# Low products behind their hi products in the attention part, and later joins at the end of each half

## The chip, the cores and the metric

The kernel runs on one core of a Trainium2 chip. The metric is the device time in microseconds, the median of several runs. One further execution was recorded by the hardware profiler, and the profile's rows are from that one.

## The reference

A bidirectional encoder of two layers over 256 tokens of width 2048, in float32:

```python
for l in range(DEPTH):                      # DEPTH = 2
    h = rms_norm(x, norm1_g[l])
    q, k, v, gu, gv = jnp.split(h @ w_in[l], splits, axis=-1)
    q = apply_rope(rms_norm(q...), cos, sin); k = apply_rope(rms_norm(k...), cos, sin)
    attn = banded_window_attention(q, k, v, sink[l])        # 8 heads of 128, 2 of k and v, |i-j| <= 128
    sgu = chunked_spatial_gating(gelu(gu), gelu(gv), ...)   # layer norm, 128x128 mixing per head, times gu
    mixed = concatenate([rms_norm(attn, ...), rms_norm(sgu, ...)])
    x = x + mixed @ w_o[l]
    x = x + conv_gated_ffn(rms_norm(x, norm2_g[l]), w_up[l], conv_w[l], conv_b[l], w_down[l])
# conv_gated_ffn: a = 3-tap convolution of h @ w_up along the tokens; g, u = split(a); (silu(g) * u) @ w_down
```

D_FF is 5632, so w_up and w_down carry most of the matmuls.

## The kernel before

Every matrix product is made of three matmuls in a rounded float format. Both factors are split: `hi` is the value rounded (a copy on ScalarE, ACT), `lo` is the rest (a subtraction on VectorE, DVE). The weight's hi part is multiplied with the activation's hi and lo part (the two "hi products"), the weight's lo part with the activation's hi part (the "low product").

Weights come in chunks of 128 x 2048 (1 MB) over SyncE's (SP) queue into `raw`, are split by `split_weights` (hi at L154, lo at L142) in pieces of a given step, and are used by one block of matmuls on TensorE (PE). There are four raw buffers, three hi buffers, three lo buffers, three PSUM accumulators `mm` and two small PSUM buffers `tp`. A buffer is let go when its last reader is done, and each engine takes its instructions in the order in which they stand in its own stream.

Four kinds of block touch the change.

- `rows_by_cols` (L181): 4 chunks of 128 rows of the weight against two token halves, 16 hi products and then 8 low products, each 512 wide. It makes the input projections (`in_rows`), the output projection (`out_rows`) and the up projection (`up_rows`).
- `unit` (L325, L330): four units a layer make the gating input gu with tokens along the free axis. A unit has two weight chunks, so two hi and two lo buffers; 32 hi products (512 wide) and then 32 low products (256 wide). Steps handed to it are run between its low products.
- The attention itself runs as a list of steps that blocks and units take in (`take`, and `let_in` for steps that wait in a list): scores (L368 to L370 on PE into a `tp` buffer, read by DVE at L558 for the masked maximum, exponentials on ACT at L580, scaling at L588), transposes of the probabilities (L596), their split (L362 on ACT, L363 on DVE) and the value products (again L368 to L370), copied out at L605.
- `direct` (L209) and `seven` (L269, L270, L275) make the down projection: plain blocks of 16 hi and 8 low products, and blocks for two column groups with seven products in place of eight. Feed-forward rows are treated in two halves; after the up projection of a half come its down blocks.

Rows of the up projection leave PSUM through `leave`: ACT scales them (L914), copies them as 16-bit words (L916), SP turns them by DMA, and some blocks later ACT joins them (L495), they are convolved (L896 on ACT, L897 and L900 on DVE), the gate's go through silu (L936), the up rows are multiplied in (L944) and the product is split (L356, L357). How many blocks later is set by `after(n, step)`: the step goes through `n` further calls of `let_in` in which it only moves up.

The order of instructions in each engine's stream is not the program's order: a scheduler works it out from priorities (`urgent()` raises them) and its own costs, and `issue_after(latest())` ties a step behind the latest matmul. A change of the program's order can so move instructions on all engines.

Of the kernel before, what the change touches and what calls it, by code (L numbers as in the profile page):

```python
# [25 lines left out]
NK = D // P  # L26
NF = DFF // P
W = 512
KB = 4
# [37 lines left out]
def encoder(ctx: ExitStack, tc: tile.TileContext, xT, x, w_in, w_gu, w_o, w_up, w_down, wsT, pcol, prow, rope, out):  # L67
# [18 lines left out]
    def ev():  # L86
        return sl([P, 2, SEQ])
# [77 lines left out]
    def after(n, step):  # L165
        waiting.append(step if n == 0 else lambda: after(n - 1, step))

    def let_in():
        for step in waiting[:]:
            waiting.remove(step)  # L170
            with tc.issue_after(latest()), urgent():
                step()


    def rows_by_cols(ps, acts, src, first, last, raw=None, apart=False, step=4 * W):

        hi, lo = split_weights(src, raw, step)

        def product(m, kk, part):
            w = (hi if part < 2 else lo)[:, kk * W : (kk + 1) * W]  # L180
            nc.tensor.matmul(  # L181
                ps[m], acts[kk][:, part % 2, m * P : (m + 1) * P], w,
                start=first and kk == 0 and part == 0, stop=last and kk == KB - 1 and part == 2,
            )

        if apart:
            for m in range(2):
                for kk in range(KB):
                    for part in range(3):
                        product(m, kk, part)  # L190
            return
        for kk in range(KB):
            for m in range(2):
                product(m, kk, 0)
                product(m, kk, 1)
            if kk == 1:
                let_in()
        for kk in range(KB):
            for m in range(2):
                product(m, kk, 2)  # L200
# [103 lines left out]
    def take(steps):  # L304
        for step in steps:
            with tc.issue_after(latest()):
                step()


    def unit(acts, w, steps=()):  # L310
        ps = mm()
        his, los = [], []
        for b in range(0, NK, UB):
            h, lo = split_weights(w[:, b * UW : (b + UB) * UW], None, 2 * W)
            his.append(h)
            los.append(lo)

        def tile_of(tiles, k, i):
            c = k % UB * UW + i * P
            return tiles[k // UB][:, c : c + P]  # L320

        for k in range(NK):
            for i in range(2):
                x1 = acts[k].rearrange("p a b -> p (a b)")
                nc.tensor.matmul(ps[:, i, :], tile_of(his, k, i), x1, start=k == 0, stop=False)  # L325
            if k == 5:
                let_in()
        for k in range(NK):
            for i in range(2):
                nc.tensor.matmul(  # L330
                    ps[:, i, :SEQ], tile_of(los, k, i), acts[k][:, 0, :], start=False, stop=k == NK - 1
                )
            if k == 0:
                take(steps)
        return ps


# [344 lines left out]
    NB = NK // KB  # L682
    for l in range(DEPTH):
        pc, qk = params
        acts = hT

        def in_rows(ps, c, b):
            src = w_in[l, c, :, b * KB * W : (b + 1) * KB * W]
            raw = first_raws.pop(0) if l == 0 and first_raws else None
            step = 2 * W if raw is None else W  # L690
            rows_by_cols(ps, acts[b * KB : b * KB + KB], src, b == 0, b == NB - 1, raw, step=step)


        psk, psq = mm(), mm()
# [27 lines left out]
        atts = []  # L722
# [41 lines left out]
        first = group_steps(0, psq)  # L764
        first()
        ps = chunk(1, [[sent_keys], [turned_keys, first], [], [first]] if l else [[], [], [sent_keys, first], [turned_keys]])
# [8 lines left out]
        for i in range(2):  # L775
# [4 lines left out]
            ps = chunk(3 + i, between[i])  # L780
# [73 lines left out]
        gates = []  # L854
# [6 lines left out]
        def out_rows(half, c, r):  # L861
            t = mm()
            ps = [t[:, m, :] for m in range(2)]
            for b in range(2):
                src = w_o[l, c, :, (half * 2 + b) * KB * W : (half * 2 + b + 1) * KB * W]
                rows_by_cols(ps, (atts, gates)[half][b * KB : b * KB + KB], src, b == 0, b == 1, step=4 * W if half else 2 * W)
            residual(ps, c, r)

        ra = inv_rms_cols(acca, D // 2, "a")
# [36 lines left out]
            src = w_up[l, n * (NF // 4) + j, :, b * KB * W : (b + 1) * KB * W]  # L906
            rows_by_cols([ps[:, m, :] for m in range(2)], acts2[b * KB : b * KB + KB], src, b == 0, b == NB - 1)

        def leave(ps, then):
            halves = []  # L910
            for m in range(2):
                rows = ev().rearrange("p a b -> p (a b)")
                with urgent():
                    nc.scalar.activation(rows, ps[:, m, :], AF.Copy, scale=r2[:, m : m + 1])  # L914
                h = sl([P, 2, 2, SEQ], U16)
                nc.scalar.copy(h, rows.bitcast(U16).rearrange("p (j n b) -> p j b n", j=2, b=2))  # L916
                halves.append(h)
            tall = [sl([P, 4, SEQ], U16) for _ in range(2)]

            def asked():  # L920
                for j in range(2):
                    for m in range(2):
                        half = halves[m][:, j, :, :].rearrange("p b n -> p (b n)")
                        nc.sync.dma_start_transpose(tall[j][:, :, m * P : (m + 1) * P], half)
                after(2, lambda: then(tall))

            waiting.append(asked)

        def gate_and_up(j, ys, mixes):
            gs = []  # L930

            def gate_in(tall):
                for i in range(2):
                    g = together(tall[i])
                    y = convolved(g, 4 * j + 2 * i)
                    nc.scalar.activation(y, y, AF.Silu)  # L936
                    gs.append(y)

            def up_in(tall):
                for i in range(2):  # L940
                    u = together(tall[i])
                    y = gs[i]
                    t = convolved(u, NF + 4 * j + 2 * i)
                    nc.vector.tensor_tensor(out=y, in0=y, in1=t, op=ALU.mult)  # L944
                    for k in range(2):
                        ys.append(split_plain(y[:, k, :]))
                    k = len(ys) - 2
                    if k in FAST[half]:
                        e = mixed(y)
                        waiting.append(lambda e=e, k=k: mixes.__setitem__(k, parts(e, [P, W])))  # L950

            if j == 0:
                pss = [mm(), mm()]
                for b in range(NB):
                    for n in range(2):
                        up_rows(pss[n], n, j, b)
                        if b == NB - 1:
                            leave(pss[n], (gate_in, up_in)[n])
                return
            for n in range(2):  # L960
                ps = mm()
                for b in range(NB):
                    up_rows(ps, n, j, b)
                leave(ps, (gate_in, up_in)[n])

        w_at = 0
        for half, (f0, f1) in enumerate(HALVES):
# [5 lines left out]
            last = f1 == NF  # L973
# [122 lines left out]
```

## Time and profile before

| | |
|---|---|
| median of three runs | 1971.12 us (1969.78 to 1973.15) |
| the profiled execution's time | 1969.81 us |
| its span in the profile | 1968.0 us |
| PE busy | 1954.8 us, 99% |
| DVE busy, ACT busy | 1334.6 us (68%), 1318.1 us (67%) |
| bytes read from HBM | 378.43 MB, 193 GB/s over the span |
| granted PE clock | full in all slices |

A row of the time lines reads: start, duration (both us), engine, line of the kernel, operation, out<-in with shapes, count, and in brackets the idle time of the engine ahead of it with what ended that. In the lists of waits: the waiting engine and line, what it waited for, us in total, times, the longest. The regions around the change: input and output projections and attention of layer 0 from the start to about 250 us, of layer 1 from about 995; the units of layer 0 from about 110 to 165, of layer 1 from about 1103 to 1158; the down blocks of the first half near 480 to 550 in layer 0 and 1460 to 1520 in layer 1.

### The profile page before, as it was taken

Reading aid. Unit: us, or ns where it says so; the run is one execution under the profiler, and the core shown is the slowest. Engines: PE = TensorE matmul, PEld = TensorE weight load, DVE = VectorE, ACT = ScalarE, POOL = GpSimd, SP = SyncE. Lnnn points to the kernel's source line nnn. Section 1 sums busy time; section 2 is a strip of 40 time slices with the busy share of each in tenths; the row PEclk is TensorE's granted clock in tenths of the full one; section 3 lists DMA queues with packets and bytes.
Section 4 is the critical chain, followed back from the end, with each engine's and each line's share of the span. In section 5 each row is a group of like instructions: output and inputs, shape, how many; then the busy total and the mean of one; then the engine's idle time right before and its main releaser. Section 6 shows DMA issues by size and latency. Waiting matters only on the chain.

```text
span 1968.0 us, 22935 instructions
## 1 busy us (share of the span) xinstructions
PE 1954.8 (99%) x8832; PEld 1622.1 (82%) x8832; DVE 1334.6 (68%) x1628; ACT 1318.1 (67%) x1437; POOL 22.9 (1%) x25
## 2 busy tenths in 40 slices
PE   9999999999999999999999999999999999999999
PEld 7878888888788888888888888888888888888887
DVE  6768775666874666688566696756668655666873
ACT  6667487687644777776666774877885456777742
POOL 0000000000000000000000000000000000000000
PEclk9999999999999999999999999999999999999999
DMA  9763486776665677757767546867766667677572
GB/s 373 218 213 141 171 235 190 220 227 195 217 235 187 217 226 223 213 174 246 231 205 221 172 150 203 242 199 222 217 197 218 214 205 223 214 217 224 169 267 86
DMA packets 190733, 414.02 MB, mean 210 GB/s; under 512 B 139424, under 2 KB 140704, under 8 KB 145568
## 3 DMA queue, kind: packets, MB, share of 16 engines
q1 hardware_dynamic: 189904, 411.83, 66.1%
q8 instruction: 69, 1.13, 0.2%
q10 hardware_dynamic: 720, 0.73, 0.1%
q14 instruction: 40, 0.33, 0.1%
HBM read 378.43 MB, written 2.10 MB: 193 GB/s over the span
## 4 chain that ended last, share of the span: by engine, by line
PE 87%; ACT 5%; DMA 3%; DVE 3%; issue 2%; SPq 0%; DVEq 0%; ACTq 0%
PE mm L181 59%; PE mm L209 17%; DMA sl<-sl 3%; PE mm L325 3%; ACT hi L154 2%; PE tp L209 2%; DVE lo L142 2%; PE mm L330 1%; ACT sl L916 1%; PE mm L275 1%; PE mm L270 1%; PE mm L269 1%; ACT sl L914 1%; ACT sl L495 1%; DVE sl L897 0%
## 5 line engine op out<-in xcount | busy, mean ns | idle before, releaser
L142 DVE TENSOR_TENSOR lo<-raw,hi 128x2048 fp32r<-128x2048 f32 (+3 forms) x444 | 839.0, 1904 | 491.0 <-ACT hi L154 442.2
L181 PE MATMUL mm<-hi,sl 128*128 128x512 f32 x3968 | 943.4, 389 | 0.9 <-ACT hi L154 0.8
L154 ACT ACTIVATE hi<-raw 128x2048 fp32r<-128x2048 f32 (+2 forms) x412 | 650.3, 1594 | 364.8 <-PE mm L181 171.7
L181 PEld LDWEIGHTS mm<-hi,sl 128*128 128x128 f32 x3968 | 744.4, 188 | 156.1 <-ACT hi L154 1.7
L181 PE MATMUL mm<-lo,sl 128*128 128x512 f32 x1984 | 491.3, 389 | 0.0
L181 PEld LDWEIGHTS mm<-lo,sl 128*128 128x128 f32 x1984 | 372.1, 188 | 76.9
L209 PE MATMUL mm<-hi,sl 128*128 128x512 f32 x1056 | 250.4, 389 | 1.9 <-ACT hi L154 1.9
L209 PEld LDWEIGHTS mm<-hi,sl 128*128 128x128 f32 x1056 | 198.1, 188 | 43.8 <-ACT hi L154 2.8
L495 ACT COPY sl<-sl 128x1024 uint16<-128x1024 uint16 x98 | 132.5, 1352 | 134.7 <-DMA sl<-sl 134.5
L209 PE MATMUL mm<-lo,sl 128*128 128x512 f32 x528 | 130.4, 389 | 0.0
L209 PEld LDWEIGHTS mm<-lo,sl 128*128 128x128 f32 x528 | 99.1, 188 | 20.5
L896 ACT ACTIVATE sl<-sl,pc 128x256 f32<-128x256 f32 x176 | 95.8, 590 | 1.3
L916 ACT COPY sl<-sl 128x1024 uint16<-128x1024 uint16 x88 | 92.0, 1046 | 2.6
L897 DVE SCALAR_TENSOR_TENSOR sl<-sl,pc 128x255 f32<-128x255 f32 x176 | 77.9, 478 | 8.1 <-ACT sl L896 8.0
L900 DVE SCALAR_TENSOR_TENSOR sl<-sl,pc 128x255 f32<-128x255 f32 x176 | 77.9, 478 | 0.7
L325 PE MATMUL mm<-sl,hi 128*128 128x512 f32 x256 | 63.7, 394 | 1.6 <-ACT sl L784 1.6
L356 ACT ACTIVATE sl<-sl 128x256 fp32r<-128x256 f32 x88 | 31.7, 408 | 46.7 <-DVE sl L944 46.7
L914 ACT ACTIVATE sl<-mm,yr 128x512 f32<-128x512 f32 x88 | 59.7, 678 | 0.0
L325 PEld LDWEIGHTS mm<-sl,hi 128*128 128x128 f32 x256 | 46.8, 188 | 10.6 <-ACT sl L784 1.8
L349 DVE SCALAR_TENSOR_TENSOR sl<-sl,pc 128x256 fp32r<-128x256 f32 x96 | 42.1, 479 | 17.6 <-ACT sl L348 17.4
L348 ACT ACTIVATE sl<-sl,pc 128x256 fp32r<-128x256 f32 x96 | 43.0, 498 | 2.3 <-DMA sl<-in_xT 1.1
L252 ACT ACTIVATE hi<-raw 128x2048 fp32r<-128x2048 f32 x16 | 30.6, 1914 | 19.2 <-PE mm L209 14.1
(144 smaller groups left out, 1062.5 us busy)
## 6 DMA issues: line engine op xcount, KB each, us to landing
raw<-in_w_up SPq DMA_DIRECT2D x176, 1024.0 KB, 5.0
raw<-in_w_down SPq DMA_DIRECT2D x88, 1024.0 KB, 4.8
raw<-in_w_in SPq DMA_DIRECT2D x38, 1024.0 KB, 5.1
raw<-in_w_o SPq DMA_DIRECT2D x32, 1024.0 KB, 5.0
raw<-in_w_gu SPq DMA_DIRECT2D x16, 1024.0 KB, 5.4
sl<-sl SPq DMA_TRANSPOSE x244, 4.3
sl<-in_prow SPq DMA_DIRECT2D x12, 256.0 KB, 7.4
raw<-in_w_in SPq DMA_DIRECT2D x8, 256.0 KB, 5.3
```

The lines of the kernel that those rows point to most:

```text
L142: nc.vector.tensor_tensor(out=lo, in0=part, in1=hi.bitcast(F32), op=ALU.subtract)
L154: nc.scalar.activation(hi[:, cs], raw[:, cs], AF.Copy)
L181: nc.tensor.matmul(ps[m], acts[kk][:, part % 2, m * P : (m + 1) * P], w, start=first and kk == 0 and part == 0, stop=last and kk == KB - 1 ...
L209: nc.tensor.matmul(ps[m], acts[kk][:, part % 2, m * P : (m + 1) * P], w, start=first, stop=done and kk == len(acts) - 1 and part == 2,)
L325: nc.tensor.matmul(ps[:, i, :], tile_of(his, k, i), x1, start=k == 0, stop=False)
L348: nc.scalar.activation(t[:, 0, :], src, AF.Copy, scale=g)
L495: nc.scalar.copy(words, tall.rearrange("p (b a) n -> p b (a n)", b=2))
L896: nc.scalar.activation(t[:, i, :], s[:, i, :], AF.Identity, bias=col(3), scale=col(1))
L897: nc.vector.scalar_tensor_tensor(out=t[:, i, 1:], in0=s[:, i, : SEQ - 1], scalar=col(0), in1=t[:, i, 1:], op0=ALU.mult, op1=ALU.add)
L900: nc.vector.scalar_tensor_tensor(out=t[:, i, : SEQ - 1], in0=s[:, i, 1:], scalar=col(2), in1=t[:, i, : SEQ - 1], op0=ALU.mult, op1=ALU.add)
L914: nc.scalar.activation(rows, ps[:, m, :], AF.Copy, scale=r2[:, m : m + 1])
L916: nc.scalar.copy(h, rows.bitcast(U16).rearrange("p (j n b) -> p j b n", j=2, b=2))
```

## The change

Three edits.

1. In `rows_by_cols`, where `in_turn` is set (all input projections, and the output projection's first half): the two low products of a row group follow its four hi products, instead of all eight low products at the end.
2. In `unit`, the low products go through all 16 rows for the first column half and then for the second, instead of alternating. The first lo buffer's last reader so is the 24th low product instead of the 16th. The steps are taken in after the second low product in both.
3. `leave` gets the number of blocks to wait, which is 3 instead of 2 for the last rows of a half.

```diff
-    def rows_by_cols(ps, acts, src, first, last, raw=None, apart=False, step=4 * W):
+    def rows_by_cols(ps, acts, src, first, last, raw=None, in_turn=False, step=4 * W):
...
         for kk in range(KB):
             for m in range(2):
                 product(m, kk, 0)
                 product(m, kk, 1)
+            if in_turn:
+                for m in range(2):
+                    product(m, kk, 2)
             if kk == 1:
                 let_in()
+        if in_turn:
+            return
         for kk in range(KB):
             for m in range(2):
                 product(m, kk, 2)
...
-        for k in range(NK):
-            for i in range(2):
+        for i in range(2):
+            for k in range(NK):
                 nc.tensor.matmul(
                     ps[:, i, :SEQ], tile_of(los, k, i), acts[k][:, 0, :], start=False, stop=k == NK - 1
                 )
-            if k == 0:
-                take(steps)
+                if i == 0 and k == 1:
+                    take(steps)
...
-            rows_by_cols(ps, acts[b * KB : b * KB + KB], src, b == 0, b == NB - 1, raw, step=step)
+            rows_by_cols(ps, acts[b * KB : b * KB + KB], src, b == 0, b == NB - 1, raw, True, step)
...
-                rows_by_cols(ps, (atts, gates)[half][b * KB : b * KB + KB], src, b == 0, b == 1, step=4 * W if half else 2 * W)
+                rows_by_cols(ps, (atts, gates)[half][b * KB : b * KB + KB], src, b == 0, b == 1, None, half == 0, 4 * W if half else 2 * W)
...
-                after(2, lambda: then(tall))
+                after(wait, lambda: then(tall))
...
-                leave(ps, (gate_in, up_in)[n])
+                leave(ps, (gate_in, up_in)[n], 2 + (j == f1 // 4 - 1))
```

(The branch `apart` of `rows_by_cols`, which nothing called, is gone too.) In the changed kernel the lines from L187 on have other numbers: L209 is L208, L325 is L324, L330 is L329, L349 is L348, L355 to L363 and L368 to L370 one less each, L495 is L494, L558 is L557, L896 is L895.

The streams of three engines move as follows. In the names, `tp_8633`, `tp_8643` hold scores of the second pair of heads' first two heads in layer 1, `tp_8738` those of the next; `lo_8960` is unit 2's second lo chunk and `lo_9084` unit 3's first; `mm_8818` is unit 1's accumulator.

DVE, units of layer 1, before:

```order
L379 TENSOR_TENSOR sl_7908<-sl_7908,sl_8591 128x512 [waits Activation_49]
L349 SCALAR_TENSOR_TENSOR sl_8594<-sl_8589,pc_2444,sl_8594 128x256 [waits Activation_49]
L349 SCALAR_TENSOR_TENSOR sl_8597<-sl_8589,pc_2444,sl_8597 128x256 [waits DMAHW4_49,Activation_49]
L558 ISA sl_8634,nmx_8632<-tp_8633,mask_121,qs_8171 128x256 [waits DMAHW5_49,PE_49]
...
L558 ISA sl_8644,nmx_8632<-tp_8643,mask_121,qs_8171 128x256 [waits DVE_49,PE_49]
...
L558 ISA sl_8739,nmx_8737<-tp_8738,mask_121,qs_8171 128x256 [waits DMAHW7_49,PE_49]
...
L142 TENSOR_TENSOR lo_8960<-raw_8957,hi_8959 128x1024 [waits DMAHW2_49,PE_49]
...
L142 TENSOR_TENSOR lo_9084<-raw_9081,hi_9083 128x1024 [waits DMAHW3_49,PE_49]
```

and in the changed kernel:

```order
L378 TENSOR_TENSOR sl_7908<-sl_7908,sl_8591 128x512 [waits Activation_49]
L142 TENSOR_TENSOR lo_8960<-raw_8957,hi_8959 128x1024 [waits DMAHW2_49,PE_49]
L142 TENSOR_TENSOR lo_8960<-raw_8957,hi_8959 128x1024
L142 TENSOR_TENSOR lo_9084<-raw_9081,hi_9083 128x1024 [waits DMAHW3_49,DVE_49,PE_49]
L142 TENSOR_TENSOR lo_9084<-raw_9081,hi_9083 128x1024
L348 SCALAR_TENSOR_TENSOR sl_8594<-sl_8589,pc_2444,sl_8594 128x256 [waits DMAHW4_49,Activation_49]
L348 SCALAR_TENSOR_TENSOR sl_8597<-sl_8589,pc_2444,sl_8597 128x256 [waits DMAHW5_49,Activation_49]
L557 ISA sl_8634,nmx_8632<-tp_8633,mask_121,qs_8171 128x256 [waits DMAHW6_49]
...
L557 ISA sl_8644,nmx_8632<-tp_8643,mask_121,qs_8171 128x256 [waits DMAHW7_49]
```

The four lo pieces have moved ahead of the L349 pair and of all reads of scores.

PE in the same place, before:

```order
L330 MATMUL mm_8818<-sl_7194,lo_8822 128x256 x2
L330 MATMUL mm_8818<-sl_7233,lo_8822 128x256 x2
L368 MATMUL tp_8738<-sl_8057,sl_8578 128x256
L369 MATMUL tp_8738<-sl_8058,sl_8578 128x256
L370 MATMUL tp_8738<-sl_8057,sl_8579 128x256
```

and in the changed kernel:

```order
L329 MATMUL mm_8818<-sl_7703,lo_8830 128x256
L329 MATMUL mm_8818<-sl_7708,lo_8830 128x256
L329 MATMUL mm_8818<-sl_7711,lo_8830 128x256
L367 MATMUL tp_8738<-sl_8057,sl_8578 128x256
L368 MATMUL tp_8738<-sl_8058,sl_8578 128x256
L369 MATMUL tp_8738<-sl_8057,sl_8579 128x256
```

The scores of the next head stood after the unit's tenth low product; they now stand after its last one.

ACT, down blocks of layer 0's first half, before (`hi_4187` and `hi_4217` belong to the third and fourth plain block, `hi_4385` and `hi_4417` to the last two, `hi_4450` to the second half's first block; `sl_4231` and `sl_4307` are the convolved up rows):

```order
L495 COPY sl_4229<-sl_4079 128x2x512 [waits DMAHW2_49,DMAHW1_49]
L896 ACTIVATE sl_4231<-sl_4229,pc_83 128x256 [waits Activation_49]
L154 ACTIVATE hi_4187<-raw_4185 128x2048 [waits DMAHW6_49,DVE_49,PE_49]
L896 ACTIVATE sl_4231<-sl_4229,pc_83 128x256
L154 ACTIVATE hi_4217<-raw_4215 128x2048 [waits DMAHW7_49,DVE_49,PE_49]
```

and in the changed kernel:

```order
L154 ACTIVATE hi_4385<-raw_4383 128x2048 [waits DMAHW7_49,DVE_49,PE_49]
L292 COPY sl_4280<-mm_4147 128x512 [waits PE_49]
L154 ACTIVATE hi_4417<-raw_4415 128x2048 [waits DMAHW0_49,DVE_49,PE_49]
L494 COPY sl_4305<-sl_4059 128x2x512 [waits DMAHW2_49,DMAHW1_49]
L895 ACTIVATE sl_4307<-sl_4305,pc_83 128x256 [waits Activation_49]
L895 ACTIVATE sl_4307<-sl_4305,pc_83 128x256
L154 ACTIVATE hi_4450<-raw_4448 128x2048 [waits DMAHW1_49,DVE_49,PE_49]
L355 ACTIVATE sl_4315<-sl_4078 128x256 [waits DVE_49]
```

The join of the up rows has moved from ahead of the third block's hi piece to behind the last block's.

More of the change, by code (lines that the diff above doesn't have):

```diff
@@ L184, in product @@
             )
[L186 to L191, printed above, removed]
         for kk in range(KB):
@@ L907, in up_rows, with leave @@
             rows_by_cols([ps[:, m, :] for m in range(2)], acts2[b * KB : b * KB + KB], src, b == 0, b == NB - 1)
-        def leave(ps, then):
+        def leave(ps, then, wait):
             halves = []
@@ L957, in gate_and_up @@
                         if b == NB - 1:
-                            leave(pss[n], (gate_in, up_in)[n])
+                            leave(pss[n], (gate_in, up_in)[n], 2)
                 return
```

## Prediction

> **What bounds the kernel now.** I read the page from its head down, then the list of TensorE's waits, then the time lines around each wait.
>
> ```profile
> span 1968.0 us, 22935 instructions
> ...
> PE 1954.8 (99%) x8832; PEld 1622.1 (82%) x8832; DVE 1334.6 (68%) x1628; ACT 1318.1 (67%) x1437; POOL 22.9 (1%) x25
> ```
>
> TensorE (PE) is busy 1954.8 of 1968.0 us, so about 13 us of idle time is all that a change of order, with the same matmuls, could ever give back. The named waits say where most of it lies:
>
> ```profile
> PE tp L369 <- DVE sl L363: 3.2, 1, 3.2
> PE mm L209 <- ACT hi L154: 1.9, 2, 1.4
> PE mm L325 <- ACT sl L784: 1.6, 1, 1.6
> PE mm L181 <- ACT hi L154: 0.8, 1, 0.8
> PE tp L368 <- DVE sl L363: 0.7, 1, 0.7
> ```
>
> (Columns: engine, operation, line waiting, what it waits for, us in total, times, longest.) These sum to 8.2 us. A gain is therefore capped near 8 us; a loss is not capped, since any new wait of PE goes straight into the span. So the question is whether the new order of VectorE (DVE) and ScalarE (ACT) makes PE wait longer somewhere.
>
> What a product costs does not change: no matmul is added or removed, and a run that stays in one accumulator has the same pitch as one that alternates (the 16 hi products of a block take 3.63 us from start to start of what follows, 0.227 each; 256-wide low products 0.12 each, both in rows below). The whole sum is waits.
>
> **The change, part by part.**
>
> *1. The start (rows by columns, low products behind their hi ones).*
>
> ```profile
> 8.65 2.42 PE L181 MATMUL mm<-hi,sl 128*128 128x512 f32 x8 [0.83 <-ACT hi L154]
> ...
> 32.78 0.87 DVE L349 SCALAR_TENSOR_TENSOR sl<-sl,pc 128x256 fp32r<-128x256 f32 x2
> ```
>
> The first block waits 0.83 us for a hi piece after eight hi products. With two low products behind each four hi ones, PE has work in that gap and ends the first block about 1.3 us earlier. The same places later depend on DVE, whose order there is unchanged: the lo halves of two activations come at 33.3 and 33.7 (second row), and PE, now 1.3 us early, waits there about 0.6. I keep −0.8 (bounds −1.3 and 0). In the steady blocks a lo buffer is needed 2.7 us earlier (after 4 products, not 16) and a hi buffer is let go 6 × 0.227 = 1.4 us later; the rows of the joins below show hi pieces made 3.5 us after ACT went idle, so that slack pays for both: nothing.
>
> *2. The units of layer 0.*
>
> ```profile
> 139.34 1.47 PE L330 MATMUL mm<-sl,lo 128*128 128x256 f32 x11
> ...
> 142.73 1.83 PE L330 MATMUL mm<-sl,lo 128*128 128x256 f32 x14
> 147.72 0.50 PE L369 MATMUL tp<-sl 128*128 128x512 f32 x1 [3.16 <-DVE sl L363]
> ...
> 151.74 0.73 PE L325 MATMUL mm<-sl,hi 128*128 128x512 f32 x2 [1.63 <-ACT sl L784]
> ```
>
> ```profile
> 142.44 4.63 DVE L142 TENSOR_TENSOR lo<-raw,hi 128x1024 fp32r<-128x1024 f32 x4 [1.64 <-PE mm L330]
> 146.99 0.68 DVE L363 TENSOR_TENSOR sl<-tp,sl 128x512 fp32r<-128x512 f32 x1
> ```
>
> Before, the largest wait is here: DVE makes four lo pieces (4.63 us) and only then the lo half of a probability tile that PE's next product needs. In the new order three such halves (about 0.6 apart) stand behind the four pieces instead of one, and four of the six value products that used to run inside the low products stand behind all 32 of them. The first buffer of the unit is let go by its 24th low product, not its 16th (8 × 0.12 = 0.96 us later). Walking it: unit 1's low products start at 139.4, the 24th ends at 142.3, they end at 143.2; DVE makes the pieces from 142.6 to 147.2 and the second half at 148.4; PE is idle from 143.2 to about 148.4 (5.2 us), and the six value products end at 149.8 instead of 148.29. The later wait of 1.63 goes with it unchanged, since its chain (ACT, from the end of those products) starts that much later. So +1.5 (bounds 0, if the halves were taken early, and +2.5).
>
> *3. The units of layer 1: the main term.*
>
> ```profile
> 1126.10 1.35 PE L330 MATMUL mm<-sl,lo 128*128 128x256 f32 x10
> ...
> 1128.85 2.68 PE L330 MATMUL mm<-sl,lo 128*128 128x256 f32 x21
> 1131.37 5.86 PE L325 MATMUL mm<-sl,hi 128*128 128x512 f32 x25
> ...
> 1149.13 0.47 PE L368 MATMUL tp<-sl 128*128 128x512 f32 x1 [0.72 <-DVE sl L363]
> ```
>
> ```profile
> 1125.10 0.87 DVE L349 SCALAR_TENSOR_TENSOR sl<-sl,pc 128x256 fp32r<-128x256 f32 x2
> 1125.89 0.47 DVE L558 CUSTOM_DVE_ANT_0 sl<-tp,mask,qs 128x256 f32<-128x256 f32 x1
> ...
> 1126.70 0.48 DVE L558 CUSTOM_DVE_ANT_0 sl<-tp,mask,qs 128x256 f32<-128x256 f32 x1
> ...
> 1129.65 1.22 DVE L142 TENSOR_TENSOR lo<-raw,hi 128x1024 fp32r<-128x1024 f32 x1
> ```
>
> Score products are written into two small PSUM buffers and read by DVE (L558). Before, DVE read the first pair at 1125.9 to 1127.5, ahead of the lo pieces at 1129.65, so that the second pair ran inside unit 1's low products. In the new order the four lo pieces lo_8960 and lo_9084 stand ahead of the first of those reads. lo_8960 can't start before the 24th low product of unit 1 and lo_9084 not before the last. The second pair (tp_8738) stands behind all 32 low products and can't start before the first pair's first tile is read. PE's work up to that point is what it was at 1131.37, less the twelve score products at 0.12 that are still to come: 1129.9, and 1130.2 with a short wait for the tile that the first pair's second half is written into. The 24th product ends 0.96 before the last, at 1129.2; DVE starts at 1129.5, takes 4.63 for the pieces (row in part 2), 0.8 for the L349 pair and 0.8 for two reads, and is done at 1135.8. PE idles 5.65 us. Then +0.2 for the second tile's reads and +0.65 at the transposes of the probabilities, whose exponentials start late; the wait of 0.72 at 1149.13 is then gone. 5.65 + 0.2 + 0.65 − 0.7 = +5.8 (bounds +4 and +7).
>
> *4. The joins of the last up projection rows.*
>
> ```profile
> 505.20 1.36 ACT L495 COPY sl<-sl 128x1024 uint16<-128x1024 uint16 x1 [5.27 <-DMA sl<-sl]
> ...
> 507.11 1.90 ACT L154 ACTIVATE hi<-raw 128x2048 fp32r<-128x2048 f32 x1
> ```
>
> ```profile
> 509.06 3.93 PE L209 MATMUL mm<-hi,sl 128*128 128x512 f32 x16 [1.37 <-ACT hi L154]
> ...
> 530.27 3.79 PE L209 MATMUL mm<-hi,sl 128*128 128x512 f32 x16
> 533.90 1.98 PE L209 MATMUL mm<-lo,sl 128*128 128x512 f32 x8
> ...
> 1484.67 3.96 PE L209 MATMUL mm<-hi,sl 128*128 128x512 f32 x16 [0.56 <-ACT hi L154]
> ```
>
> ```profile
> 528.66 1.92 ACT L154 ACTIVATE hi<-raw 128x2048 fp32r<-128x2048 f32 x1 [1.63 <-PE mm L209]
> 534.10 1.93 ACT L154 ACTIVATE hi<-raw 128x2048 fp32r<-128x2048 f32 x1 [3.52 <-PE mm L209]
> ```
>
> ```profile
> 529.37 2.28 DVE L142 TENSOR_TENSOR lo<-raw,hi 128x2048 fp32r<-128x2048 f32 x1
> ...
> 532.17 2.28 DVE L142 TENSOR_TENSOR lo<-raw,hi 128x2048 fp32r<-128x2048 f32 x1
> ```
>
> Before, ACT waits 5.27 us for the turned rows, and the hi piece behind it makes PE wait 1.37 (0.56 in layer 1). Those waits go: −1.9. But queued behind the moved joins are now hi pieces of blocks that PE reaches at once, and the chain of copy, convolution, multiply and split runs beside DVE's lo pieces at 529 to 534, where DVE has no idle time. The last two blocks of the pair use its result; the new PE order mixes them with the next half's first block, product by product, so PE has other work. Walking it in times 1.37 earlier: hi_4450 is ready 0.35 after PE wants it, the first split tiles come 0.2 late on ACT and 0.2 on DVE, the second pair 0.65 late. That is 1.4 a layer, +2.8, against −1.9: +0.9 (bounds −1.9, all hidden, and +5.5, when the mixed-in products don't cover and each layer loses 3.7). Half 1 has three more blocks in between; nothing there.
>
> **Sum:** −0.8 + 1.5 + 5.8 + 0.9 = +7.4 us on the profiled execution's 1969.81, which is 1977.2; on the median of the runs, 1971.12, it is 1978.5. I say 1978.
>
> [...] The longest idle of PE before is 3.16 us, and the products behind it run at the usual pitch at a granted clock of 1.00. [...]
>
> **Rivals.**
> - *Nothing to measure.* The score tiles' wait is not there: DVE would have to be done with the lo pieces when PE comes to tp_8738. For it: DVE is only 68% busy. Against it: the pieces can't start before a product that PE does one microsecond earlier, and 4.63 us of work is in the row. Without the main term +1.6, 1972.7.
> - *Faster.* The listed waits at L181, L209, L369 and L325 go and nothing comes: −7.5, 1963.6. For it: three of the four lie where the order changed. Against it: at L369 more now stands behind the same lo pieces.
> - *The joins stall in full* at the last two blocks of half 0: +7.4 − 2.8 + 7.4 = +12, 1983.
> - *The clock falls behind the long idles.* If the pitch of 0.227 doubles for a stretch as long as the idle that has left no trace (3.16 us), each loses 1.6, together +10.6, 1981.7; speaking against it, 3.16 us left nothing.
>
> **How the numbers follow.** Forecast 0.54, clock 0.11, joins in full 0.10, nothing 0.16, faster 0.09. A measurement of this kernel tells about 0.2%, 3.9 us, from no change. Forecast, clock and joins give slower, except for the low tail of the first (about 0.06, when the main term is +4 and the joins are hidden): slower 0.69; the tail and the second rival give same 0.22; faster 0.09. The range runs from the "nothing" case to the joins' case: 1971.5 to 1984. The forecast's own range is 1974 to 1981.
>
> **What would show it.** PE's list of waits should have one wait of 5 to 6 us at L367 for DVE L557 near 1130, behind unit 1's low products; one of about 5 at L367 or L368 for L362 near 143; none at 509 and 1485; small ones (under 1 us) at L208 near 535 and 541. It is wrong if DVE shows the L557 reads ahead of the lo pieces in time, if PE's wait near 1130 is under 3 us, or if a wait over 1 us appears in the steady blocks at L181, where I put nothing.

## The result, and the profile after

The changed kernel takes 1980.19 us (median of 5 executions, 1979.56 to 1981.24). The kernel before, on the same chip, takes 1972.19 us (5 executions, 1969.78 to 1973.15). The ratio is 1.0044, with a 95% interval of 1.0033 to 1.0055: slower by 8.0 us. The forecast was 1978.0 us in a range from 1971.5 to 1984. Of all executions in this document one was slow, one of the kernel with the second edit alone (2815.67 us at a mean granted clock of 0.654); it is left out of that kernel's ratio.

The head of the page of the changed kernel:

```profile
span 1979.2 us, 22930 instructions
...
PE 1960.0 (99%) x8832; PEld 1625.5 (82%) x8832; DVE 1331.6 (67%) x1628; ACT 1317.2 (67%) x1437; POOL 20.4 (1%) x25
```

PE has as many matmuls as before, 8832, but is busy 1960.0 us and not 1954.8. So 5.2 us of the loss is not waiting: the same products took longer. PE's list of waits (engine, line waiting, what it waits for, us in total, times, longest):

```profile
PE tp L367 <- DVE nmx L557: 5.4, 1, 5.4
PE tp L367 <- DVE sl L362: 5.1, 1, 5.1
PE mm L181 <- DVE sl L348: 1.5, 2, 1.2
...
PE mm L181 <- ACT hi L154: 0.8, 1, 0.8
PE mm L324 <- ACT sl L783: 0.8, 1, 0.8
```

The first two are the waits that the prediction put at 5.65 and 5.2 us. The 3.2 and 0.7 us of the list before are gone, of the 1.9 at the down blocks 0.4 is left, and the 0.8 at L181 is still there. Next the two places in PE's time line (start, duration, line, operation, count, and in brackets the idle time and what ended it), first the units of layer 0, then those of layer 1:

```profile
149.90 0.77 PE L367 MATMUL tp<-sl 128*128 128x512 f32 x1 [5.06 <-DVE sl L362]
150.46 0.63 PE L368 MATMUL tp<-sl 128*128 128x512 f32 x1
150.88 0.63 PE L369 MATMUL tp<-sl 128*128 128x512 f32 x1
...
156.08 0.73 PE L324 MATMUL mm<-sl,hi 128*128 128x512 f32 x2 [0.75 <-ACT sl L783]
...
1132.93 1.36 PE L329 MATMUL mm<-sl,lo 128*128 128x256 f32 x10
1139.65 0.58 PE L367 MATMUL tp<-sl 128*128 128x256 f32 x1 [5.37 <-DVE nmx L557]
1140.03 0.41 PE L368 MATMUL tp<-sl 128*128 128x256 f32 x1
1140.24 0.41 PE L369 MATMUL tp<-sl 128*128 128x256 f32 x1
...
1142.38 4.84 PE L324 MATMUL mm<-sl,hi 128*128 128x512 f32 x15
```

and DVE at the same two places:

```profile
143.92 4.63 DVE L142 TENSOR_TENSOR lo<-raw,hi 128x1024 fp32r<-128x1024 f32 x4 [1.59 <-PE mm L329]
148.47 0.68 DVE L362 TENSOR_TENSOR sl<-sl 128x512 fp32r<-128x512 f32 x1
149.07 1.28 DVE L362 TENSOR_TENSOR sl<-tp,sl 128x512 fp32r<-128x512 f32 x2
...
1133.37 4.63 DVE L142 TENSOR_TENSOR lo<-raw,hi 128x1024 fp32r<-128x1024 f32 x4
1137.92 0.87 DVE L348 SCALAR_TENSOR_TENSOR sl<-sl,pc 128x256 fp32r<-128x256 f32 x2
1138.71 0.47 DVE L557 CUSTOM_DVE_ANT_0 sl<-tp,mask,qs 128x256 f32<-128x256 f32 x1
```

The chain is the one forecast: four lo pieces (4.63 us) stand in DVE's stream ahead of what PE's next product needs, the lo halves of the split probabilities from 148.47 on in layer 0 and the score reads from 1138.71 on in layer 1.

The rows of PE also show what was not in the sum. Behind each wait, 512-wide products start 0.42 us apart (150.46 to 150.88) and 256-wide ones 0.21 apart, where the rows before have 0.227 and 0.12. The windows of the same execution (stretch, its length, then busy time and count of PE, PEld, DVE, ACT and POOL, granted PE clock, DMA share, GB/s) say why:

```profile
148.00:150.00 2.00, 0.10 (x1) 0.14 (x1) 2.00 (x4) 0.00 (x0) 0.00 (x0) 0.59 0.93 381
150.00:152.00 2.00, 2.00 (x5) 1.61 (x6) 0.34 (x1) 0.00 (x0) 0.00 (x0) 0.50 1.01 406
...
154.00:156.00 2.00, 1.33 (x7) 1.06 (x5) 1.49 (x5) 2.00 (x6) 0.00 (x0) 0.71 0.00 0
...
1136.00:1138.00 2.00, 0.00 (x0) 0.00 (x0) 2.00 (x3) 0.48 (x1) 0.00 (x0) 1.00 0.59 143
1138.00:1140.00 2.00, 0.35 (x1) 0.35 (x2) 2.00 (x9) 0.00 (x0) 0.00 (x0) 0.55 1.02 426
...
1144.00:1146.00 2.00, 2.00 (x8) 1.55 (x7) 1.93 (x9) 1.74 (x3) 0.00 (x0) 0.74 0.01 4
```

The granted clock is halved late in each wait and stays so for some 5 us of work. In layer 0 that costs six 512-wide products 0.2 us each and twelve 256-wide ones 0.093 each, 2.3 us; in layer 1 twelve at 0.093 and 1.27 us in the fifteen products from 1142.38, 2.4 us.

Set side by side by the starts of the same products, the later execution falls behind the earlier one like this (us):

| stretch | prediction | the two profiled executions |
|---|---|---|
| start, up to unit 1's low products (139.34, now 140.84) | −0.8 | +1.5 |
| units of layer 0 (151.74, now 156.08) | +1.5 | +2.8 |
| from there to the joins of layer 0 | | +0.2 |
| joins of layer 0 | with layer 1's +0.9 | −1.15 |
| units of layer 1 | +5.8 | +8.05 |
| joins of layer 1 | | −0.35 |
| sum | +7.4 | +11.1 |

The two profiled executions are 11.4 us apart (1969.81 and 1981.18), the medians 8.0. That the recorded execution of before lies 2.4 us under its median is part of the story, below.

### The profile page after: what moved, and what is told of

It reads as the page before. It is cut to its first block, busy times and chain, and to the rows that moved or that the text cites. A ratio compares the mean times of both kernels' runs of the same rounds, so it can differ in the third digit from the quotient of the medians.

```text
span 1979.2 us, 22930 instructions
## 1 busy us (share of the span) xinstructions
PE 1960.0 (99%) x8832; PEld 1625.5 (82%) x8832; DVE 1331.6 (67%) x1628; ACT 1317.2 (67%) x1437; POOL 20.4 (1%) x25
## 4 chain that ended last, share of the span: by engine, by line
PE 96%; DVE 1%; ACT 1%; DMA 0%; issue 0%; SPq 0%; DVEq 0%
PE mm L181 66%; PE mm L208 18%; PE mm L324 3%; PE tp L208 2%; PE mm L329 1%; PE mm L269 1%; PE mm L274 1%; PE mm L268 1%; PE tp L367 0%; DVE lo L142 0%; PE tp L369 0%; PE tp L595 0%; PE tp L368 0%; PE tp L811 0%; PE tp L274 0%; PE tp L268 0%
## 5 line engine op out<-in xcount | busy, mean ns | idle before, releaser
L181 PE MATMUL mm<-hi,sl 128*128 128x512 f32 x3968 | 970.1, 389 | 2.3 <-DVE sl L348 1.5
L181 PEld LDWEIGHTS mm<-hi,sl 128*128 128x128 f32 x3968 | 743.6, 188 | 157.6 <-DVE sl L348 3.0
L181 PE MATMUL mm<-lo,sl 128*128 128x512 f32 x1984 | 517.7, 389 | 0.0
L181 PEld LDWEIGHTS mm<-lo,sl 128*128 128x128 f32 x1984 | 372.3, 188 | 77.5 <-DVE lo L142 0.3
L208 PE MATMUL mm<-hi,sl 128*128 128x512 f32 x1056 | 250.4, 389 | 0.4 <-ACT hi L154 0.4
L208 PEld LDWEIGHTS mm<-hi,sl 128*128 128x128 f32 x1056 | 198.1, 188 | 42.3 <-ACT hi L154 1.2
L494 ACT COPY sl<-sl 128x1024 uint16<-128x1024 uint16 x98 | 132.3, 1350 | 116.5 <-DMA sl<-sl 116.5
L208 PE MATMUL mm<-lo,sl 128*128 128x512 f32 x528 | 130.4, 389 | 0.0
L208 PEld LDWEIGHTS mm<-lo,sl 128*128 128x128 f32 x528 | 99.1, 188 | 20.5
L895 ACT ACTIVATE sl<-sl,pc 128x256 f32<-128x256 f32 x176 | 95.6, 590 | 1.2
L896 DVE SCALAR_TENSOR_TENSOR sl<-sl,pc 128x255 f32<-128x255 f32 x176 | 77.0, 478 | 4.2 <-ACT sl L895 4.2
L324 PE MATMUL mm<-sl,hi 128*128 128x512 f32 x256 | 65.4, 399 | 0.8 <-ACT sl L783 0.8
L355 ACT ACTIVATE sl<-sl 128x256 fp32r<-128x256 f32 x88 | 31.7, 407 | 50.3 <-DVE sl L943 50.3
L324 PEld LDWEIGHTS mm<-sl,hi 128*128 128x128 f32 x256 | 48.0, 192 | 10.2 <-ACT sl L783 1.0
L348 DVE SCALAR_TENSOR_TENSOR sl<-sl,pc 128x256 fp32r<-128x256 f32 x96 | 41.9, 479 | 15.8 <-ACT sl L347 15.8
```

What stands on the lines that cost most here:

```text
L181: nc.tensor.matmul(ps[m], acts[kk][:, part % 2, m * P : (m + 1) * P], w, start=first and kk == 0 and part == 0, stop=last and kk == KB - 1 ...
L208: nc.tensor.matmul(ps[m], acts[kk][:, part % 2, m * P : (m + 1) * P], w, start=first, stop=done and kk == len(acts) - 1 and part == 2,)
L494: nc.scalar.copy(words, tall.rearrange("p (b a) n -> p b (a n)", b=2))
L895: nc.scalar.activation(t[:, i, :], s[:, i, :], AF.Identity, bias=col(3), scale=col(1))
L896: nc.vector.scalar_tensor_tensor(out=t[:, i, 1:], in0=s[:, i, : SEQ - 1], scalar=col(0), in1=t[:, i, 1:], op0=ALU.mult, op1=ALU.add)
```

## The experiments

**The theories.** *Order of DVE:* the first edit lets the scheduler put the lo pieces ahead of the score reads and probability halves; both long waits come from that, and the half clock from the waits. *Late release:* the second edit lets go of the first lo buffer 8 products later, and the waits come from that. *Own cost:* the new order of the products costs time by itself, at L181 and in the units.

Where an experiment starts from the kernel before, its lines have the numbers of before; the first one alone was made from the changed kernel by taking the other two edits back, so its lines have the changed kernel's numbers.

**The first edit alone.** The kernel before with

```diff
+            if in_turn:
+                for m in range(2):
+                    product(m, kk, 2)
...
+        if in_turn:
+            return
...
```

and the calls that set `in_turn`.

> Only the first edit: low products behind their hi ones in the input and output projections; units and joins as before. In this kernel's DVE stream lo_8960 and lo_9084 stand ahead of the reads of tp_8633, and lo_1507 and lo_1637 ahead of three lo halves, as in the changed kernel. Theory 'DVE order' (the two long waits of 5.1 and 5.4 us come from where the lo pieces stand in DVE's stream, and the clock halves behind them): both waits are there, each within 1 us of the changed kernel's, with granted clock 0.50 behind each; the joins' waits of 1.4 and 0.6 stay; +9 to +11 us. Rival 'late release' (the waits come from the unit's first lo buffer being let go at the 24th low product, which is undone here): the waits shrink to below 3.5 us, no clock loss; 0 to +3 us.

Measured: 1977.66 us against 1970.77, ratio 1.0036 (1.0024 to 1.0048), +6.9 us. Its two longest waits of PE:

```profile
PE tp L367 <- DVE nmx L557: 5.0, 1, 5.0
PE tp L367 <- DVE sl L362: 4.1, 1, 4.1
```

Both long waits are there without the second edit, which lengthens them by 0.4 and 1.0 us (to 5.4 and 5.1). So the order of DVE comes from the first edit, and the late release adds about what 8 products at 0.12 us are, as far as it adds anything. The time is below the 9 to 11 us that were expected: in layer 0 the clock is halved for about 3.5 us (worked out from a granted clock of 0.97 over 130 to 147 and 0.90 over 147 to 160) and not for 6.8 as in the changed kernel, and of the joins' waits of 1.37 and 0.56 one of 0.56 is left (at 509.21).

**The second edit alone.** The kernel before with

```diff
-        for k in range(NK):
-            for i in range(2):
+        for i in range(2):
+            for k in range(NK):
...
-            if k == 0:
-                take(steps)
+                if i == 0 and k == 1:
+                    take(steps)
```

> Only the second edit: the unit's low products by column half. In this kernel's DVE stream the reads of the score tiles stand ahead of the lo pieces, as in the kernel before. Theory 'DVE order': no wait above 4.2 us, no clock loss; the wait of 3.16 near 147 grows by up to 0.96 (the pieces start at the 24th low product, if it is still what DVE waits for); 0 to +1.5 us. Rival 'late release': waits of about 5 us at both places and a halved clock, +7 to +9 us.

Measured: 1975.63 us against 1970.77, ratio 1.0027 (1.0017 to 1.0037), +4.9 us: between the two theories' numbers, and for another reason than either gave. From its list of waits:

```profile
PE tp L369 <- DVE sl L363: 3.6, 1, 3.6
PE mm L209 <- ACT hi L154: 2.6, 2, 1.7
PE tp L812 <- issue: 2.3, 1, 2.3
```

The wait at L369 grew from 3.2 to 3.6, and a new one came at L812, where the gating's normalised rows go in. The list puts it down to "issue". DVE, in that stretch, has six lo pieces (1158.31 to 1162.9 and 1164.85 to 1167.2) and behind them a last read of a `tp` buffer (L363, 1167.72 to 1168.40); PE's first product at L812, which writes into a `tp` buffer, starts at 1168.50. That PE waits for this read to let the buffer go is argued from the order and the times, not shown. The rows that DVE still normalises there (L831, to 1169.00) end too late for that first product to have waited for them. Two windows there:

```profile
1165.02:1168.43 3.41, 1.22 (x6) 0.68 (x4) 3.41 (x5) 0.60 (x2) 0.00 (x0) 1.00 0.90 308
1168.43:1171.84 3.41, 3.34 (x12) 3.08 (x13) 2.42 (x5) 0.00 (x0) 0.00 (x0) 0.50 0.73 288
```

The clock was halved behind an idle of 2.3 us, shorter than the 3.16 us that left nothing in the kernel before's recorded execution. The two edits don't add up: alone they cost 6.9 and 4.9 us, all three together 8.0, and the wait at L812 is not in the changed kernel's list.

**The joins alone.** The kernel before with

```diff
-                after(2, lambda: then(tall))
+                after(wait, lambda: then(tall))
...
-                leave(ps, (gate_in, up_in)[n])
+                leave(ps, (gate_in, up_in)[n], 2 + (j == f1 // 4 - 1))
```

> Only the third edit: the joins of each half's last rows one block later. In the changed kernel PE's waits at the joins came to 0.2 to 0.4 in all in place of 1.9. Theory 'joins gain': waits of 1.37 and 0.56 gone, 0.2 new in each layer; -1.5 us (-1.0 to -1.9), which 5 rounds may just tell from nothing. Rival (the prediction's, even or a loss because DVE and ACT are late for the last two blocks): 0 to +1.5 us.

Measured: 1970.97 us against 1970.77, ratio 1.0002 (0.9993 to 1.0010): no difference, where 1.0 to 1.9 us less was expected. The waits of 1.37 and 0.56 us are gone (0.4 in two waits at L209 is left), but the median doesn't show it. This execution's wait in layer 0, and two windows around it:

```profile
147.54 0.72 PE L369 MATMUL tp<-sl 128*128 128x512 f32 x1 [3.17 <-DVE sl L363]
```

```profile
144.23:147.65 3.42, 0.25 (x3) 0.12 (x2) 3.25 (x4) 0.00 (x0) 0.00 (x0) 1.00 0.56 120
147.65:151.06 3.41, 3.41 (x14) 3.10 (x14) 0.66 (x2) 2.31 (x5) 0.00 (x0) 0.50 0.97 348
```

The wait is the one of the kernel before to a hundredth, 3.17 against 3.16, but here the clock is halved behind it. In the recorded execution of before the windows of that length lie otherwise (where their edges come from is told in the last section):

```profile
142.72:146.13 3.41, 1.85 (x15) 1.63 (x13) 3.41 (x4) 0.00 (x0) 0.00 (x0) 1.00 0.19 24
146.13:149.55 3.42, 1.82 (x11) 1.57 (x12) 1.54 (x2) 1.03 (x2) 0.00 (x0) 1.00 0.85 345
```

An edge at 146.13 cuts the wait in two, and PE is busy for more than half of either window. So the recorded execution of before, with 1.00 throughout, is one of several ways in which that wait can end. Over the 39 executions of the kernel before in two of the comparisons (with this one and with the kernels from the reads on) the mean clock was 0.997 to 1.000 and the time 1968.85 to 1975.31; the 14 with a mean clock of 0.999 or 1.000 have a median of 1969.8 us, the 25 below of 1972.07.

**The second edit and the joins**, the first one left out:

> The changed kernel without its first edit. Theory 'DVE order': the sum of the two before, -1.9 to +0.5 us, no wait above 4.2 us and granted clock 1.00 throughout. Rival 'late release': +5 to +8 us.

Measured: 1975.8 us against 1970.77, ratio 1.0022 (1.0013 to 1.0032). That is not what the theory of DVE's order expected, and at the edge of its rival's range, but without the rival's waits of 5 us: the waits of 3.6 and 2.3 us are those of the second edit alone, the clock is halved for some 10.2 us from 147.1 on (0.52 over 147 to 149, 0.50 from 149 to 157, 0.92 over 157 to 159), and the joins bring nothing here either. Taking the first edit out of the changed kernel thus recovers about 3 us of 8, not all.

**The changed kernel, its score reads put first on DVE.**

```diff
+                  with urgent():
                     nc.vector.tensor_tensor_reduce(
```

> The changed kernel with all three edits; DVE's reads of the scores (L557) get the scheduler's raised priority, and in this kernel's DVE stream the reads of tp_8633 and tp_8643 stand ahead of lo_8960 and lo_9084 again. The order in layer 0 is as in the changed kernel. Theory 'DVE order': the wait of 5.4 us in layer 1 is gone, and with it the half clock behind it (2.3 us), so about 7 us faster than the changed kernel: +1 to +2.5 us against the kernel before; the wait of 5.1 near 145 stays. Rival 'DVE has too much to do there' (the lo pieces are then late in turn): a new wait of 3 us or more for lo_8960 or lo_9084 in layer 1, +4 to +8 us.

Measured: 1972.04 us against 1972.07, ratio 1.0002 (0.9993 to 1.0011). The 8 us are gone with one line that changes no product. Two of its waits of PE:

```profile
PE tp L367 <- DVE sl L362: 5.1, 1, 5.1
...
PE mm L324 <- ACT sl L784: 0.7, 1, 0.7
```

and in layer 1, where the changed kernel waited 5.37 us, PE is busy throughout at the full clock:

```profile
1130.00:1140.00 10.00, 9.97 (x56) 8.62 (x56) 9.74 (x24) 6.24 (x11) 0.00 (x0) 1.00 0.18 53
```

That settles the main term: the reads' place behind the lo pieces is its cause, and it is worth some 7.5 to 8 us. From unit 1's first low product to the first product behind the units it takes 32.47 us here (1126.87 to 1159.34) and 40.02 in the changed kernel (1129.36 to 1169.38); the wait of 5.37 and 2.4 of half clock are nearly all of that. The whole kernel is at least 1 us better than was expected.

**The idle in layer 0 filled.** The changed kernel with 36 products by zeros, 256 wide, behind unit 1's low products in layer 0 (they add nothing to the sums):

```diff
...
+        for f in range(fill):
+            nc.tensor.matmul(ps[:, 1, :SEQ], none, acts[f % NK][:, 0, :], start=False, stop=f == fill - 1)
...
```

> The changed kernel, and in layer 0 alone 36 more products of 256 columns by a tile of zeros at the end of unit 1 (4.3 us of PE work that changes no value), in PE's order just ahead of the wait of 5.06 us; nothing else moves on any engine. Theory 'clock' (an idle PE gets half the clock for about 5 us): the wait shrinks to about 0.7 us, the granted clock stays at 1.00 there and the span from unit 1's first low product to the first hi product of unit 2 shortens by 2 to 2.5 us though PE does 4.3 us more; -2 to -2.5 us against the changed kernel. Rival 'the slow products have another cause' (transfers or PSUM contention at that time): the products behind the wait are slow as before; no change (within 0.5 us).

Measured: 1978.34 us (1976.9 to 1979.43) against 1972.07, ratio 1.0034 (1.0021 to 1.0047). PE there:

```profile
142.44 4.48 PE L339 MATMUL mm<-sl,none 128*128 128x256 f32 x36
147.66 0.47 PE L373 MATMUL tp<-sl 128*128 128x512 f32 x1 [0.74 <-DVE sl L368]
147.97 0.40 PE L374 MATMUL tp<-sl 128*128 128x512 f32 x1
...
152.56 0.73 PE L327 MATMUL mm<-sl,hi 128*128 128x512 f32 x2 [1.64 <-ACT sl L789]
```

With PE kept busy, the products behind it start 0.23 us apart and the clock is 1.00 from 140 to 160. From unit 1's first low product to unit 2's first hi product it takes 13.95 us (138.61 to 152.56), in the changed kernel 15.24 (140.84 to 156.08). The 2.3 us of half speed are gone; 0.9 of them come back, as the wait for ACT at unit 2 grows from 0.75 to 1.64. So here the half clock came with the idle and went with it, and of the price of that, part lay beside a later wait: 1.29 us are gained at the place, where 2 to 2.5 were expected.

**The kernel before with the later joins, and the split halves first on DVE.**

```diff
-                pT.append(parts(t.rearrange("p a b -> p (a b)"), [P, W]))
+                with urgent():
+                    pT.append(parts(t.rearrange("p a b -> p (a b)"), [P, W]))
```

> The kernel before with the third edit (joins later), and the split of the turned probabilities (L362 and L363) at raised priority: in DVE's stream all three lo halves stand ahead of lo_1507 and lo_1637 in layer 0. Theory 'DVE order': the wait of 3.16 us near 147, which is in the kernel before, shrinks to under 1 us, and with it the half clock that stands behind it in some executions; -3 to -6 us against the kernel before. Rival 'the stall moves on' (the four lo pieces, now later, make PE wait at unit 2's low products): -1 to +1 us.

Measured: 1962.4 us (1962.29 to 1963.68) against 1972.07, ratio 0.9956 (0.9943 to 0.9968). This beats both kernels, by 9.7 and by some 18 us, and what was expected (3 to 6 us). All its named waits of PE:

```profile
PE tp L120 <- DVE ones L116: 1.1, 1, 1.1
PE mm L181 <- ACT hi L154: 0.7, 1, 0.7
PE mm L209 <- ACT hi L154: 0.4, 2, 0.2
PE tp L370 <- DVE sl L363: 0.2, 1, 0.2
```

Its five executions lie within 1.4 us, where those of the kernel before spread over 4.6 (1969.24 to 1973.81) in the same comparison.

**The halves first, without the later joins.**

> The kernel before, with only the split halves of the turned probabilities (L362, L363) put ahead of the weight pieces in VectorE's stream; the joins stay as they were. If the wait of 3.16 us and the half clock behind it are what the order of VectorE cost the kernel before, nearly all of the 9.7 us of the run with the later joins is here: 1963 to 1965, with the waits of 1.37 and 0.56 us at the down blocks still listed. If the joins gave a good part of it, 1966 to 1970.

Measured: 1967.66 us (1964.1 to 1969.97) against 1970.72, ratio 0.9982 (0.9973 to 0.9991). That is only 3.1 of the 9.7 us: the second of the two expectations holds, that the joins gave a good part of it. PE at the first down block behind the joins, and ACT ahead of it:

```profile
506.39 6.34 PE L209 MATMUL mm<-hi,sl 128*128 128x512 f32 x16 [3.61 <-ACT hi L154]
512.57 1.99 PE L209 MATMUL mm<-lo,sl 128*128 128x512 f32 x8
```

```profile
502.57 1.33 ACT L495 COPY sl<-sl 128x1024 uint16<-128x1024 uint16 x1 [5.77 <-DMA sl<-sl]
```

PE came to this block some 5 us earlier than in the kernel before (its wait began at 502.8, before at 507.7), but the turned rows that ACT joins came 2.6 us earlier only (502.57, before 505.20). The wait grew from 1.37 to 3.61 us, the products behind it were slow (16 in 6.18 us, usually 3.63, with a mean granted clock of 0.998 over this execution), and most of the gain was handed back. With the later joins ACT no longer waits there, so that edit is worth about 5 to 6.6 us once PE is early (1967.66 to 1962.4 in two comparisons, or 3.1 against 9.7 us under the kernel before of each), and nothing that can be measured while it is late.

**The changed kernel with both put first.** Score reads and split halves in `urgent()`:

> The changed kernel with the score reads (L557) and the split halves of the turned probabilities put ahead of the weight pieces on VectorE. If the loss is VectorE's order alone and none of it the new order of the products itself, both long waits go and the time is that of the kernel before with the same repair and the later joins, 1962 to 1964. If the order of the products costs something of its own (steady blocks at L181, the units), it stays at 1966 or more.

Measured: 1970.75 us against 1970.72, ratio 0.9999 (0.9990 to 1.0008). The expectation is missed because the edit did not reach its place: with the new order of the products, the three halves of layer 0 still stand behind the four pieces, and the wait is unchanged:

```profile
PE tp L367 <- DVE sl L362: 5.1, 1, 5.1
PE mm L324 <- ACT sl L785: 1.3, 1, 1.3
```

These two and 1.8 us of half clock make 8.2 us. The span is 8.1 us over the 1960.6 of the kernel with joins and halves first.

**The same, with the first edit only in layer 1's input projections** (and the output projections), so that the halves of layer 0 do move:

```diff
-            rows_by_cols(ps, acts[b * KB : b * KB + KB], src, b == 0, b == NB - 1, raw, True, step)
+            rows_by_cols(ps, acts[b * KB : b * KB + KB], src, b == 0, b == NB - 1, raw, l == 1, step)
```

> As the changed kernel with both score reads and split halves put first on VectorE, but with the low products behind their hi ones only in layer 1's input projections (and the output projections): in this order the split halves of layer 0 really stand ahead of the weight pieces, which they did not in the run before. If the whole remaining loss was that one wait of 5.06 us with the half clock and the 1.3 us behind it, about 8 us, this gives 1962 to 1965. If the order of the products costs time of its own, or the second edit brings the wait for the spatial rows (2.3 us and a half clock) back, 1966 to 1970.

Measured: 1964.97 us (1964.64 to 1967.98) against 1971.13, ratio 0.9973 (0.9963 to 0.9983). What is left of its waits:

```profile
PE mm L324 <- ACT sl L785: 1.6, 1, 1.6
PE mm L181 <- ACT hi L154: 1.3, 2, 0.7
```

All three edits are in this kernel (the first without layer 0's input projections), and it is some 14 to 15 us faster than the changed one. To the fastest kernel 2.6 us are left by the medians and 3.5 by the differences from the kernel before in each comparison, and the 1.6 at L324 and the 0.6 more at L181 are 2.2 of them. So an "own cost" of the order of the products is at most about 1 us for what is in this kernel. For the first edit in layer 0's input projections it stays open, since no run here has it together with the halves ahead of the pieces.

## Why the prediction was right, and where it was not

**What bounds the kernel.** Right in the main. A change of order that gives DVE's work another place moves the time by what PE then waits, and, as the runs add, by the clock behind some of these waits (2.3 and 2.4 us here). What failed is "What a product costs does not change": with the same 8832 matmuls PE is busy 5.2 us longer.

**Part 1, the start: −0.8, in this execution +1.5.** The gain came and was lost again. The wait of 0.8 at L181 stayed, but a block that started at 29.08 before starts at 28.28, which is 0.80 earlier. Then two new waits for L348 add 1.5 us, and unit 1's low products start 1.5 us late: in this execution a row of parameters landed late, and DVE stood still for it:

```profile
28.07 0.17 DVE L461 TENSOR_SCALAR nsink<-qk 128x8 f32<-128x8 f32 x1 [5.59 <-DMA qk<-in_prow]
```

(26.20 before.) The four other profiled executions with the first edit in layer 0 have no such waits. Unit 1's low products start at 137.98 to 138.61 in them, and at 138.75 to 139.97 in the seven without that edit. So a gain of about 1 us is the edit's, and the loss is this execution's. That PE would wait at the lo halves was in the text, at 0.6; the 1.19 us of the longer of the two waits stand there and not in the steady blocks, where a wait over 1 us would have spoken against the prediction.

**Part 2, layer 0: +1.5, measured +2.8.** The walk was right: 5.2 us of idle forecast, 5.06 measured, products and split halves in the forecast order. What failed is "the later wait of 1.63 goes with it unchanged": it shrank to 0.75, and 2.3 us of half clock, which the sum left out, came instead.

**Part 3, layer 1: +5.8, measured +8.0.** The wait was forecast at 5.65 and is 5.37. The mis-sized term is again the clock, 2.4 us in the products from 1140.03 to 1147.06. That the wait's cause is the order of DVE is shown by the run with the reads put first, which takes 8 us back.

**Part 4, joins: +0.9, measured −1.5 in these executions.** The waits went, as forecast. The losses of 1.4 a layer behind them did not come: one wait of 0.20 us in each layer is all, at 538.95 and at 1522.27. The first of them:

```profile
538.95 9.38 PE L208 MATMUL mm<-hi,sl 128*128 128x512 f32 x40 [0.20 <-ACT hi L154]
```

Alone, this edit gives nothing that can be measured. Why the 1.9 us of removed waits don't show in the median is open; the executions of both kernels scatter by 4 us and more, with mean clocks of 0.997 to 1.000.

**The clock.** The prediction had it as a rival, at 0.11 and with 10.6 us in all, and drew "3.16 us left nothing" from one execution. It happened, with the forecast's waits: two idles above 5 us, each with 6.8 us at half speed that cost 2.3 to 2.4 us, where the rival had 3.16 us at half speed that cost 1.6. That the time came out so near the forecast is luck in good part. A clock loss of 4.7 us that the sum left out met a loss of 2.8 at the joins that did not come and a later wait that fell by 0.9, and the kernel before has a clock loss of its own in most executions (25 of 39 have a mean clock of 0.998 or less), so that the medians are 8.0 us apart and not 11.4.

## What to carry to other kernels

When one edit changes the order of a bound engine's work, ask first what it does to the streams of the engines that serve it: here edits of PE's order moved the time through two places in DVE's stream, and one line of priority took all of it back. Put the small work that the bound engine waits for ahead of the big pieces that it needs only later. Waits of 2.3 to 5.4 us on TensorE had stretches of half clock behind them here, 3.4 to 10.2 us long, and one of 3.16 us had none. Price a wait with such a stretch, and a gain ahead of a place that waits for a transfer with what that wait gives back.

## What the runs showed of the hardware

- The clock was halved behind idles of 5.37 and 5.06 us (the changed kernel), 3.6 and 2.3 us (the second edit alone) and 3.17 us (the joins alone), to 0.50 each time, and stayed at 1.00 behind one of 3.16 us (the kernel before). So in these runs the length of the idle alone did not decide.
- The half-speed stretches run from 148.34 to 155.17 and from 1138.21 to 1145.03 in the changed kernel, 6.8 us each, and from 1168.43 to 1171.84 in the kernel with the second edit alone, 3.4 us. In the changed kernel's trace the clock changes once more, behind the last product, at 1977.88. Its five changes lie 0, 6.83, 989.87, 996.69 and 1829.54 us behind the first, 0, 2, 290, 292 and 536 times 3.413 us, and its clock record begins at 4.98 us, 42 such steps ahead of the first. The two idles begin at 144.84 and 1134.28, which are 0.09 and 0.5 us ahead of such a step. The windows of the kernel before that stand above are cut by the same length: its clock record begins at 6.19 us, and 40, 41 and 42 steps on are 142.72, 146.13 and 149.55.
- Cut at these steps, the two places of the changed kernel read like this (columns as above, the busy time of PE first behind the length):

```profile
144.93:148.34 3.41, 0.00 (x0) 0.00 (x0) 3.41 (x4) 1.46 (x3) 0.00 (x0) 1.00 0.29 50
148.34:151.75 3.41, 1.85 (x5) 1.50 (x6) 2.00 (x4) 0.00 (x0) 0.00 (x0) 0.50 1.01 416
151.75:155.17 3.42, 3.42 (x15) 3.11 (x13) 0.66 (x2) 2.31 (x5) 0.00 (x0) 0.50 0.36 149
155.17:158.58 3.41, 2.66 (x14) 2.11 (x14) 3.41 (x11) 2.86 (x6) 0.00 (x0) 1.00 0.00 0
...
1134.79:1138.21 3.42, 0.00 (x0) 0.00 (x0) 3.42 (x4) 1.68 (x2) 0.00 (x0) 1.00 0.40 110
1138.21:1141.62 3.41, 1.97 (x9) 1.97 (x10) 2.80 (x13) 0.98 (x4) 0.00 (x0) 0.50 1.02 411
1141.62:1145.03 3.41, 3.41 (x12) 2.83 (x12) 3.41 (x14) 3.38 (x10) 0.00 (x0) 0.50 0.23 94
1145.03:1148.45 3.42, 3.42 (x21) 2.90 (x20) 2.47 (x12) 0.81 (x3) 0.70 (x1) 1.00 0.00 0
```

- Behind both windows without a matmul the next one ran at half speed. At half speed, the windows that the matmuls filled to 0.54 and 0.58 were followed by another at half speed, those filled to 1.00 by one at full speed. A third window before a fall, at the end of that trace (1974.47 to 1977.88), was filled to 0.30. All other whole windows at full clock in this trace and in that of the kernel before were followed by full clock; the least filled of them had 0.72 (28.88 to 32.29) and 0.52 (149.55 to 152.96).
- The wait of 3.16 us lay across two windows filled to 0.54 and 0.53. That of 3.17 us left its window filled to 0.07, and the one of 2.3 us to 0.36, and both were followed by half speed. So in the windows named here those ahead of a fall were filled to 0.36 or less, and those at full clock ahead of none to 0.52 or more. In the case of 2.3 us PE was busy for 1.22 us of the window ahead of the fall. No run here varied the moment of an idle on purpose; where it fell among the windows was chance.
